# A two-block transformer kernel on one Trainium2 core: the second mixer's value products, all eight chunks of the first half of tokens ahead of the second half

## The chip, the core and the metric

The kernel runs as one program on one core of a Trainium2 chip. The core has engines that run side by side, each through its own list of instructions in order: TensorE (PE in the rows below; its loading of weights is PEld) multiplies matrices into PSUM, VectorE (DVE) and ScalarE (ACT) work elementwise, GpSimd (POOL) does a few small jobs, and SyncE (SP) issues the DMAs that bring weights from HBM to SBUF. Semaphores tie the lists together. The metric is device time of one execution in microseconds (us), the median of several; lower is better.

## The reference

The input is 256 tokens of width 1024. A first block (a recurrent mixer, a sparse attention and a gated embedding) is followed by two layers of the same form, `i` = 0 and 1:

```
mod = (silu(c) @ mod_w[i] + mod_b[i]) as six vectors of 1024
y   = mixer(x * (1 + mod[1]) + mod[0])            # i = 0: MLA, i = 1: MoBA
x   = layer_norm(ALPHA * x + mod[2] * y)
y   = conv_ffn(x * (1 + mod[4]) + mod[3])
x   = layer_norm(ALPHA * x + mod[5] * y)
```

The mixer of layer 1 (MoBA, with one block of 256 keys here) is causal attention with 8 heads of 128, with queries, keys and values from one 1024x3072 weight. What this document is about lies between the feed-forward part of layer 0 and the heads of layer 1: the layer norm between them, the values of the second mixer, and two of the modulation vectors, `mod[4]` and `mod[3]` of layer 1, which nobody needs before the layer norm behind the second mixer.

## The kernel before, in words

Every activation is kept as two parts, high and low, whose sum is the float32 value, and so is every weight. A weight chunk is 128 input channels by 1024 columns. Its DMA puts two chunks (1 MB) into one of six buffers `raw`. ACT makes the high part (`split`, L174), DVE the low part (L175), into one of four pairs of buffers `wh` and `wl`; with more than four chunks in a group, both parts of the others share a buffer `ws`, which is taken from the six of `raw`. A product of tokens by weight then costs three matmuls (`mm3t`, L213 to L215): high by high, high by low, and low by high, so L215 alone needs the low part of the activation.

**Halves.** Tokens go through a layer in two halves of 128, `tb` = 0 and 1. `tokens` calls `halves` once for each group of chunks; `halves` makes the splits of the whole group and then issues the matmuls, first all of the group for the first half, then for the second. The value products of the second mixer (`mobav`) had the groups [0, 1, 2, 3], [4, 5] and [6, 7]. Eight chunks, two halves, two column blocks of 512 and three terms make 96 matmuls.

**The layer norm in front.** When the feed-forward products of a half (`ps_fy`) are done, DVE adds the residual and takes the moments (L1084 to L1087), POOL makes the inverse deviation, DVE and ACT normalize half a row each (L1114, L1115). `feed` then turns the result into the mixer's input chunk by chunk: PE transposes (L367), ACT writes the high part `ln` (L372) and, for every second chunk, the scaled value (L376; DVE for the others, L374), DVE writes the low part (L377). `Norm.emit` says in which order: chunks 0 to 3 of the first half when that half is ready, and everything else after the second half is ready.

**Modulation units.** A modulation vector is four units of work, each with a DMA of 1 MB (`raw_mod`), and an end (`fin`: a sum with the bias in `modr`, two transposes `ps_modt`, a copy `mod`). A unit is done on PE (`mm`: eight matmuls of 32 rows by 256 columns, L983) or on DVE (`add`: four passes over 1024 columns, the first one of a vector on ACT, L996 and L998); if a vector had units on DVE, four more matmuls with `ones` bring their sum `modacc` into the same PSUM tile. `bg` takes the next unit from a queue. `fetch` and `units`, called by `halves` with `fill`, load some units early. Before, `fill` was 5 at the end of layer 0's feed-forward part: the last unit of `mod[4]` and all four of `mod[3]` of layer 1. The heads of the second mixer call `bg` once a step as long as `mod[3]` is missing.

The order of the instructions on each engine is set by a scheduler when the kernel is built; it keeps dependencies and the `issue_after` edges of the code, and otherwise moves work.

Of the kernel before, what the change touches and what calls it, by code (L numbers as in the profile page):

```python
# [21 lines left out]
KD = D // P  # L22
F = 2816
NF = F // P
# [23 lines left out]
class G:  # L48
# [7 lines left out]
    def __init__(self, ctx, tc, a):  # L56
        self.tc, self.nc, self.a = tc, tc.nc, a
        pool = lambda n, **kw: ctx.enter_context(tc.tile_pool(name=n, bufs=1, **kw))
        self.cp = pool("cp")
        self.sp = pool("stream")  # L60
        self.rp = pool("res")
        self.pp = pool("pp", space=PSUM)
        self.dp = pool("dp", space=DRAM)
        self.modrow = {}
        self.pending, self.marks, self.fed = None, [], {}
        self.queue, self.early, self.have = [], [], set()
# [960 lines left out]
def affine(g, name, gain, shift, scale, offset):  # L1027

    V = g.nc.vector
    s1, b1 = g.col(8, name + "s"), g.col(8, name + "b")  # L1030
    V.scalar_tensor_tensor(s1, scale, 1.0, gain, op0=ALU.add, op1=ALU.mult)
    if shift is None:
        V.tensor_copy(b1, offset)
    else:
        V.scalar_tensor_tensor(b1, scale, 1.0, shift, op0=ALU.add, op1=ALU.mult)
        V.tensor_tensor(b1, b1, offset, op=ALU.add)
    return s1, b1


class Norm:  # L1040


    def __init__(self, g, name, joint=False):
        self.g, self.name, self.joint = g, name, joint
        self.x = g.xs(name)
        self.r = [None, None]

    def emit(self, g, xh, tb, aff):
        self.r[tb] = xh
        lo, hi = list(range(4)), list(range(4, KD))  # L1050
        if self.joint:
            todo = [((0, 1), lo + hi)] if tb else []
        else:
            todo = [((1,), lo), ((0,), hi), ((1,), hi)] if tb else [((0,), lo)]
        for tbs, ks in todo:
            g.feed(self.r, tbs, ks, *aff, self.x, self.name)
# [18 lines left out]
def residual_moments(g, name, z, acc, cols, scale, after):  # L1075

    V = g.nc.vector
    st, mv = g.col(18, f"{name}st"), g.col(2, f"{name}mv")
    with ExitStack() as ctx:
        for ins in after:  # L1080
            ctx.enter_context(g.tc.issue_after(ins.ins))
        for n, c in enumerate(cols):
            t = g.b2(f"{name}t{n}")[:, 0:c.stop - c.start]
            V.tensor_tensor(t, acc(n), scale[:, c], op=ALU.mult)  # L1084
            V.scalar_tensor_tensor(z[:, c], z[:, c], ALPHA, t, op0=ALU.mult, op1=ALU.add)
            V.bn_stats(st[:, 6 * n:6 * n + 6], z[:, c])
        V.bn_aggr(mv, st[:, 0:6 * len(cols)])  # L1087
    return mv[:, 0:1], mv[:, 1:2]


def rstd(g, name, var):
    v = g.col(1, f"{name}v")
    g.nc.vector.tensor_scalar(v, var, LN_EPS, None, op0=ALU.add)
    return g.rsqrt(v, f"{name}r")


def resid_ln(g, i, j, prev, nxt, name):

    nc, a = g.nc, g.a
    V, A = nc.vector, nc.scalar  # L1100
    scale = g.row(g.modrow[i, (2, 5)[j]], name + "m")
    gain, shift = (g.row(a[n][i, j:j + 1, :], name + n) for n in ("ln_g_2", "ln_b_2"))
    out = Norm(g, name, j == 0)
    aff = affine(g, name + "a", g.ln_g[:, i, j, :], g.ln_b[:, i, j, :], *nxt)

    def done(tb, acc):
        z, h = prev[tb], f"{name}{tb}"
        cols = TAIL if tb and out.joint else N512
        after = g.marks if tb and not out.joint else ()
        mean, var = residual_moments(g, h, z, lambda n: acc(tb, n), cols, scale, after)  # L1110
        r = rstd(g, h, var)
        nr = g.col(1, f"{h}nr")
        iv = V.scalar_tensor_tensor(nr, mean, -1.0, r, op0=ALU.mult, op1=ALU.mult)
        V.tensor_scalar(z[:, 0:512], z[:, 0:512], mean, r, op0=ALU.subtract, op1=ALU.mult)  # L1114
        A.activation(z[:, 512:1024], z[:, 512:1024], AF.Identity, bias=nr, scale=r)  # L1115
        if out.joint == bool(tb):
            g.marks = [iv]
        out.emit(g, z, tb, aff)

    out.rows = gain, shift  # L1120
    return out, done
# [201 lines left out]
def moba(g, x, ln, early):  # L1323
    nc, a = g.nc, g.a
    A, T, V = nc.scalar, nc.tensor, nc.vector
    w = a["moba_w_in_2"][0]

    vacc = g.pair("mobav")
    vt = [g.b4(f"mobav{tb}") for tb in range(2)]

    def vdone(tb):
        for n, c in enumerate(N512):
            A.copy(vt[tb][:, c], vacc(tb, n))

    g.tokens(w, x, [[0, 1, 2, 3], [4, 5], [6, 7]], vacc, vdone, "mobav", c0=2048)
    g.flush()
    rest = early()
    q, k = [], []

    def units():  # L1340
        for hp in range(4):
            for m, ps in g.proj(w, 256 * hp, 2, x, f"mobaq{hp}", wide=True):
                q.append(g.t1(f"mobaq{2 * hp + m}"))
                g.added(ps, f"mobaq{2 * hp + m}", q[-1], 128.0 ** -0.5 * 2.0 ** (2 * hp + m + 1))
                yield
            for m, ps in g.proj(w, 1024 + 256 * hp, 2, x, f"mobak{hp}", wide=True):
                k.append(g.t1(f"mobak{2 * hp + m}"))
                g.added(ps, f"mobak{2 * hp + m}", k[-1])
                yield

    proj = units()
    for _ in range(5):
        next(proj)

    def fill(st):
        for _ in range(2):
            next(proj, None)
        if st >= 1 and rest:
            rest.pop(0)(g.smr)
        if (1, 3) not in g.have:  # L1360
            g.bg()

    def logits(h, out, tb):
        n = (tb + 1) * P
        T.matmul(out, q[h][:, tb * P:n], k[h][:, 0:n], start=True, stop=True)

    o = heads(g, "moba", logits, g.dist, lambda h: 2.0 ** -(h + 1), vt, "V", fill)
    n, done = ln()
    acc = g.pair("mobay")
    part = lambda tb, n: acc(tb, n, (N512, TAIL)[tb][n].stop - (N512, TAIL)[tb][n].start)  # L1370
    g.tokens(a["moba_w_o_2"][0], o, [[0, 1], [2, 3], [4, 5, 6, 7]], part, lambda tb: done(tb, part), "mobay", fill=4, by_column=True)
    return n


def ffn(g, i, x, ln, early):
    nc, a = g.nc, g.a
    V, A = nc.vector, nc.scalar
    w, wo = a["ffn_w_in_2"][i], a["ffn_w_out_2"][i]
    cw, cb = g.ffc[i], g.ffb[i]
    hid = [None] * NF  # L1380
# [39 lines left out]
    todo = [0, 2]  # L1420
    last = NF - (6, 8)[i]
    acc = g.pair(f"fy{i}", third="V")
    width = N512, TAIL if i else N512
    part = lambda tb, n: acc(tb, n, width[tb][n].stop - width[tb][n].start)
    load = g.loader(wo, 0, D, f"fo{i}_")
    ends = 0, NF - 1
    for c in range(4, NF, 2):
# [26 lines left out]
        if c == NF - 4:  # L1454
            n, done = ln()
        while todo[0] < min(c, last):
# [1 line left out]
            ks = [k for k in (m, m + 1) if k < last]  # L1458
            g.halves(load, ks, hid, part, width, f"fo{i}_", ends)
            todo = todo[1:]  # L1460
    g.halves(load, list(range(last, NF)), hid, part, width, f"fo{i}_", ends, lambda tb: done(tb, part), 0 if i else 5, i == 1)
    return n


# [55 lines left out]
```

## Time and profile before

| what | before |
|---|---|
| median of 3 runs | 877.28 us (877.24 to 877.99) |
| the profiled execution's own time | 879.18 us |
| its span, first to last instruction | 877.4 us |
| PE busy | 859.3 us, 98% |
| DVE busy | 673.2 us, 77% |
| ACT busy | 502.6 us, 57% |
| DMA read from HBM | 197.28 MB, 226 GB/s over the span |

The span is what the rows below measure in; 1.8 us of the execution's own time lie around it. Times in rows count from the span's start. Idle time of an engine stands in square brackets with what ended it. "PEclk" is the share of full speed that TensorE's clock was granted: 1.00 is 2.4 GHz, 0.50 is 1.2 GHz.

### The profile page before, as it was taken

The numbers are of one execution on the slowest core, as the hardware profiler recorded it, in microseconds if no ns is written. First come the engines' busy times: TensorE is split into PE (matmuls) and PEld (weight loads), VectorE is DVE, ScalarE is ACT, GpSimd is POOL, SyncE is SP. The second block draws the span as 40 slices with busy tenths as digits, with TensorE's granted clock in tenths as the row PEclk, the third lists the DMA queues.
The fourth block names the chain that finished last, engine by engine and source line by source line (L and its number), as shares of the span: only waits on it lengthen the run. The fifth ranks groups of instructions, "written<-read, shape, count | busy, mean of one in ns | idle before, by whom it ended". The sixth has DMA issues, their size and how long they took to land. (4 is left out here: it accounts for less than half of the span.)

```text
span 877.4 us, 14288 instructions
## 1 busy us (share of the span) xinstructions
PE 859.3 (98%) x5415; PEld 741.1 (84%) x5415; DVE 673.2 (77%) x1289; ACT 502.6 (57%) x925; POOL 52.6 (6%) x81
## 2 busy tenths in 40 slices
PE   9999999999999899999999999999999999999996
PEld 8998779999888688798888888678888988888885
DVE  5798787768767576679899998675866686777786
ACT  6555666445557555377556557276553775565660
POOL 2003111000000131000000000000000000000003
PEclk9999999999999999999999999999999999999999
DMA  8955796854447963498898985498453956566411
GB/s 269 357 197 175 279 345 202 285 211 151 144 150 258 305 250 117 132 377 286 305 331 296 336 290 190 162 345 296 161 176 104 377 178 203 181 220 204 143 49 48
DMA packets 112760, 199.27 MB, mean 227 GB/s; under 512 B 8388, under 2 KB 76468, under 8 KB 112692
## 3 DMA queue, kind: packets, MB, share of 16 engines
q1 hardware_dynamic: 111892, 196.25, 65.7%
q0 software_dynamic: 496, 1.59, 0.5%
q8 instruction: 42, 0.69, 0.3%
q10 hardware_dynamic: 304, 0.53, 0.2%
q14 instruction: 26, 0.21, 0.1%
HBM read 197.28 MB, written 1.08 MB: 226 GB/s over the span
## 5 line engine op out<-in xcount | busy, mean ns | idle before, releaser
L194 PE MATMUL ps_f<-ln,wh_f 128*128 128x512 f32 x576 | 203.8, 396 | 0.0
L195 PE MATMUL ps_f<-ln,wl_f 128*128 128x256 f32 x576 | 161.4, 280 | 0.0
L194 PEld LDWEIGHTS ps_f<-ln,wh_f 128*128 128x128 f32 x576 | 108.1, 188 | 26.5 <-issue 0.8
L195 PEld LDWEIGHTS ps_f<-ln,wl_f 128*128 128x128 f32 x576 | 108.7, 189 | 1.4 <-issue 0.4
L174 ACT CAST wh_fo<-raw_fo 128x1024 fp32r<-128x1024 f32 x38 | 39.9, 1050 | 39.3 <-PE ps_f L194 38.2
L174 ACT CAST wh_f<-raw_fa 128x1024 fp32r<-128x1024 f32 x36 | 37.7, 1051 | 40.8 <-PE ps_f L194 20.3
L175 DVE TENSOR_TENSOR wl_fo<-raw_fo,wh_fo 128x1024 fp32r<-128x1024 f32 x38 | 46.5, 1223 | 19.0 <-ACT wh_fo L174 18.9
L175 DVE TENSOR_TENSOR wl_f<-raw_fa,wh_f 128x1024 fp32r<-128x1024 f32 x36 | 43.9, 1222 | 15.3 <-ACT wh_f L174 15.3
L174 ACT CAST wh_f<-raw_fb 128x1024 fp32r<-128x1024 f32 x36 | 37.1, 1050 | 28.0 <-PE ps_fy L215 17.8
L998 DVE SCALAR_TENSOR_TENSOR modacc<-raw_mod,c,modacc 128x1024 f32<-128x1024 f32 x40 | 51.1, 1278 | 2.0 <-ACT modacc L996 2.0
L175 DVE TENSOR_TENSOR wl_f<-raw_fb,wh_f 128x1024 fp32r<-128x1024 f32 x36 | 43.4, 1221 | 9.2 <-ACT wh_f L174 8.9
L188 PE MATMUL ps_fi<-ln,wh_fi 128*128 128x256 f32 x128 | 35.6, 285 | 0.0
L215 PE MATMUL ps_fy<-wh_fo,fh 128*128 128x512 f32 (+1 forms) x99 | 35.2, 369 | 0.0
L214 PE MATMUL ps_fy<-wl_fo,fh 128*128 128x512 f32 (+1 forms) x99 | 35.1, 368 | 0.0
L189 PE MATMUL ps_fi<-ln,wl_fi 128*128 128x256 f32 x128 | 34.6, 283 | 0.0
L187 PE MATMUL ps_fi<-ln,wh_fi 128*128 128x256 f32 x128 | 34.0, 286 | 0.0
L213 PE MATMUL ps_fy<-wh_fo,fh 128*128 128x512 f32 (+1 forms) x99 | 33.3, 367 | 0.0
L204 DVE TENSOR_TENSOR adf<-ps_f,adf 128x256 f32<-128x256 f32 x72 | 30.0, 417 | 0.0
L983 PE MATMUL ps_mod<-raw_mod,c 128*32 128x256 f32 x400 | 26.9, 383 | 1.0 <-DVE mod L1013 1.0
L203 ACT COPY adf<-ps_f 128x256 f32<-128x256 f32 x72 | 26.1, 363 | 0.0
L174 ACT CAST wh_fi<-raw_fi 128x1024 fp32r<-128x1024 f32 x16 | 17.0, 1079 | 14.9 <-PE ps_mlay L215 8.3
L188 PEld LDWEIGHTS ps_fi<-ln,wh_fi 128*128 128x128 f32 x128 | 24.5, 192 | 0.4 <-DVE ln L377 0.4
(807 smaller groups left out, 2582.4 us busy)
## 6 DMA issues: line engine op xcount, KB each, us to landing
raw_mod<-in_mod_w_dram SPq DMA_DIRECT2D x48, 1024.0 KB
raw_fo<-in_ffn_w_out_dram SPq DMA_DIRECT2D x22, 1024.0 KB
raw_fa<-in_ffn_w_in_dram SPq DMA_DIRECT2D x18, 1024.0 KB
raw_fb<-in_ffn_w_in_dram SPq DMA_DIRECT2D x18, 1024.0 KB
raw_fi<-in_ffn_w_in_dram SPq DMA_DIRECT2D x16, 512.0 KB
raw_wo<-in_w_out_dram SPq DMA_DIRECT2D x6, 1024.0 KB
raw_aqk<-in_w_in_dram SPq DMA_DIRECT2D x4, 1024.0 KB
raw_mqk<-in_w_in_dram SPq DMA_DIRECT2D x4, 1024.0 KB
```

The lines of the kernel that those rows point to most:

```text
L174: self.nc.scalar.copy(hv, src)
L175: self.nc.vector.tensor_tensor(lv, src, hv.bitcast(F32), op=ALU.subtract)
L187: T.matmul(ps, wh, xh, start=start, stop=False, skip_group_check=chk)
L188: T.matmul(ps, wh, xl, start=False, stop=False, skip_group_check=chk)
L189: T.matmul(ps, wl, xh, start=False, stop=stop, skip_group_check=chk)
L194: T.matmul(ps, wh, x[2], start=start, stop=False, skip_group_check=True)
L195: T.matmul(ps[:, 0:S], wl, x[0], start=False, stop=stop, skip_group_check=True)
L204: V.tensor_tensor(t, ps[:, 0:S], t, op=ALU.add)
L213: T.matmul(ps, xh, wh, start=start, stop=False)
L214: T.matmul(ps, xh, wl, start=False, stop=False)
L215: return T.matmul(ps, xl, wh, start=False, stop=stop)
L998: nc.vector.scalar_tensor_tensor(st["acc"], rv[:, e], c, st["acc"], op0=ALU.mult, op1=ALU.add)
```

## The change

Three edits. The value products become one group of eight chunks, so all 48 matmuls of the first half stand ahead of those of the second, and chunks 4 to 7 of the weight are kept in `ws` buffers. The layer norm in front feeds each half whole, as soon as that half is ready. And of the five modulation units at the end of the feed-forward part one stays; the other four (`mod[3]`) go to the first four steps of the heads, by turns on DVE and on PE.

```diff
@@ class Norm
-    def __init__(self, g, name, joint=False):
-        self.g, self.name, self.joint = g, name, joint
+    def __init__(self, g, name, joint=False, whole=False):
+        self.g, self.name, self.joint, self.whole = g, name, joint, whole
...
         if self.joint:
             todo = [((0, 1), lo + hi)] if tb else []
+        elif self.whole:
+            todo = [((tb,), lo + hi)]
         else:
             todo = [((1,), lo), ((0,), hi), ((1,), hi)] if tb else [((0,), lo)]
@@ def resid_ln
-    out = Norm(g, name, j == 0)
+    out = Norm(g, name, j == 0, j == 1)
@@ def moba
-    g.tokens(w, x, [[0, 1, 2, 3], [4, 5], [6, 7]], vacc, vdone, "mobav", c0=2048)
+    g.tokens(w, x, [list(range(KD))], vacc, vdone, "mobav", c0=2048)
...
         if (1, 3) not in g.have:
-            g.bg()
+            g.bg(tensor=st % 2 == 1)
@@ def ffn
-    g.halves(..., lambda tb: done(tb, part), 0 if i else 5, i == 1)
+    g.halves(..., lambda tb: done(tb, part), 0 if i else 1, i == 1)
```

Two lines are added ahead of these places, so a line of the kernel before has a number two higher in the changed one from L1054 on.

How this moves instructions. On PE, right behind the last feed-forward product, before (`ps_mod` are modulation units, `ps_ln` the transposes of the feed, `x_72` and `x_73` the two halves):

```order
L215 MATMUL ps_fy_4894<-ws_fo_21_6224,fo_21l 128x512
L983 MATMUL ps_mod_6349<-raw_mod_6227,c 32x256 x6
L367 MATMUL ps_ln_6292<-ident,x_72 128x128 x4
L983 MATMUL ps_mod_6349<-raw_mod_6227,c 32x256 x2
L983 MATMUL ps_mod_6349<-modacc_5899,ones 32x256 x4
L1011 MATMUL ps_modt_6791<-ident,modr_6787 128x128 x2
L983 MATMUL ps_mod_6796<-raw_mod_6229,c 32x256 x8
L983 MATMUL ps_mod_6796<-raw_mod_6231,c 32x256 x8
L983 MATMUL ps_mod_6796<-raw_mod_6233,c 32x256 x8
L983 MATMUL ps_mod_6796<-raw_mod_6235,c 32x256 x3
L367 MATMUL ps_ln_6425<-ident,x_73 128x128 x4
```

and in the changed kernel, at the same place:

```order
L983 MATMUL ps_mod_6362<-modacc_5899,ones 32x256 x3
L213 MATMUL ps_mobav_6409<-wh_mobav_6375,ln_6066 128x512
L214 MATMUL ps_mobav_6409<-wl_mobav_6376,ln_6066 128x512
L213 MATMUL ps_mobav_6413<-wh_mobav_6375,ln_6066 128x512
L214 MATMUL ps_mobav_6413<-wl_mobav_6376,ln_6066 128x512
L1011 MATMUL ps_modt_6779<-ident,modr_6775 128x128 x2
L215 MATMUL ps_mobav_6409<-wh_mobav_6375,ln_6066 128x512
L215 MATMUL ps_mobav_6413<-wh_mobav_6375,ln_6066 128x512
L213 MATMUL ps_mobav_6409<-wh_mobav_6379,ln_6066 128x512
L214 MATMUL ps_mobav_6409<-wl_mobav_6380,ln_6066 128x512
L213 MATMUL ps_mobav_6413<-wh_mobav_6379,ln_6066 128x512
L214 MATMUL ps_mobav_6413<-wl_mobav_6380,ln_6066 128x512
```

Ahead of these rows stand one unit, one matmul with `ones` and eight transposes of the first half. Four units are gone, and the value products begin; the first low-part matmuls (L215) stand behind the two transposes of `modr`.

On DVE, behind the normalizing of the first half (`x_72`), before; `ln_6066` is the low part of chunk 0 and then of chunk 1:

```order
L1114 TENSOR_SCALAR x_72<-x_72,ln010mv,ln010ry 128x512
L1084 TENSOR_TENSOR ln011t_6408<-ps_fy_4887,row_ln01m 128x512
L1085 SCALAR_TENSOR_TENSOR x_73<-x_73,ln011t_6408 128x512
L1084 TENSOR_TENSOR ln011t_6412<-ps_fy_4894,row_ln01m 128x512
L1086 BN_STATS ln011st<-x_73 128x6
L1085 SCALAR_TENSOR_TENSOR x_73<-x_73,ln011t_6412 128x512
L1008 SCALAR_TENSOR_TENSOR modr_6787<-ps_mod_6349,modb_6788 128x256
L1086 BN_STATS ln011st<-x_73 128x6
L377 TENSOR_TENSOR ln_6066<-ln01f_6297,ln_6066 128x128
```

and in the changed kernel, from there to the low part of chunk 0:

```order
L1116 TENSOR_SCALAR x_72<-x_72,ln010mv,ln010ry 128x512
L175 TENSOR_TENSOR wl_mobav_6380<-raw_mobav_6373,wh_mobav_6379 128x1024
L175 TENSOR_TENSOR wl_mobav_6386<-raw_mobav_6383,wh_mobav_6385 128x1024
L175 TENSOR_TENSOR wl_mobav_6390<-raw_mobav_6383,wh_mobav_6389 128x1024
L1086 TENSOR_TENSOR ln011t_6461<-ps_fy_4887,row_ln01m 128x512
L1086 TENSOR_TENSOR ln011t_6465<-ps_fy_4894,row_ln01m 128x512
L175 TENSOR_TENSOR ws_mobav_6395<-raw_mobav_6393,ws_mobav_6395 128x1024
L175 TENSOR_TENSOR ws_mobav_6398<-raw_mobav_6393,ws_mobav_6398 128x1024
L1008 SCALAR_TENSOR_TENSOR modr_6775<-ps_mod_6362,modb_6776 128x256
L1087 SCALAR_TENSOR_TENSOR x_73<-x_73,ln011t_6461 128x512
L377 TENSOR_TENSOR ln_6066<-ln01f_6289,ln_6066 128x128
```

Five weight splits now stand between the normalizing and that low part. (One more stands ahead of the moments' `BN_AGGR` of the first half.) The rows that follow in the changed kernel, to the low part of chunk 1:

```order
L1087 SCALAR_TENSOR_TENSOR x_73<-x_73,ln011t_6465 128x512
L374 TENSOR_SCALAR ln01f_6293<-ps_ln_6284,ln01as,ln01ab 128x128
L175 TENSOR_TENSOR ws_mobav_6403<-raw_mobav_6401,ws_mobav_6403 128x1024
L175 TENSOR_TENSOR ws_mobav_6406<-raw_mobav_6401,ws_mobav_6406 128x1024
L1013 COPY mod_6782<-ps_modt_6779 128x2x4
L1088 BN_STATS ln011st<-x_73 128x6 x2
L377 TENSOR_TENSOR ln_6066<-ln01f_6293,ln_6066 128x128
```

The last two splits and the moments of the second half stand ahead of it; before, four short rows lie between those two low parts.

## Rows read from the trace of the kernel before

**Rows 1.** The page's first part: busy time, share of the span, instructions.

```profile
PE 859.3 (98%) x5415; PEld 741.1 (84%) x5415; DVE 673.2 (77%) x1289; ACT 502.6 (57%) x925; POOL 52.6 (6%) x81
```

**Rows 2.** Stretches: length, busy time (instructions) by engine, PEclk, DMA share, GB/s.

```profile
562.85:572.88 10.03, 8.76 (x108) 4.77 (x107) 7.12 (x21) 5.63 (x11) 0.55 (x1) 1.00 0.95 340
572.88:594.99 22.11, 22.11 (x98) 18.05 (x98) 15.16 (x28) 16.26 (x29) 0.00 (x0) 1.00 1.04 345
609.00:650.20 41.20, 41.20 (x252) 36.75 (x251) 32.44 (x84) 25.49 (x57) 0.00 (x0) 1.00 0.53 180
650.20:682.40 32.20, 31.41 (x216) 24.98 (x214) 19.62 (x48) 11.93 (x25) 1.21 (x2) 1.00 0.39 132
```

**Rows 3.** Timeline of PE: start, length, instruction, count, idle before.

```profile
562.62 0.40 PE L215 MATMUL ps_fy<-ws_fo,fo_21l 128*128 128x512 f32 x1
...
567.29 3.22 PE L983 MATMUL ps_mod<-raw_mod,c 128*32 128x256 f32 x54 [0.74 <-DVE mod L1013]
570.44 1.53 PE L367 MATMUL ps_ln<-ident,x 128*128 128x128 f32 x12
571.90 1.05 PE L983 MATMUL ps_mod<-raw_mod,c 128*32 128x256 f32 x10
...
594.99 0.62 PE L194 MATMUL ps_mobaq<-ln,wh_mobaq 128*128 128x512 f32 x2
```

**Rows 4.** SP's issues and ACT around the first value weights, same columns.

```profile
550.39 0.37 SPq L159 DMA_DIRECT2D raw_mod<-in_mod_w_dram  x1
...
563.04 0.37 SPq L159 DMA_DIRECT2D raw_mobav<-in_moba_w_in_dram  x1
...
564.63 0.46 ACT L372 ACTIVATE ln<-ps_ln,ln01ab,ln01as 128x128 fp32r<-128x128 f32 x1 [4.39 <-PE ps_ln L367]
...
570.38 1.99 ACT L174 CAST wh_mobav<-raw_mobav 128x1024 fp32r<-128x1024 f32 x2 [0.98 <-DMA raw_mobav<-in_moba_w_in_dram]
```

**Rows 5.** The DMA engines from 556.5 to 562.3, columns of rows 2.

```profile
556.50:562.30 5.80, 5.80 (x27) 4.71 (x26) 3.27 (x8) 0.81 (x1) 0.55 (x1) 1.00 0.00 0
```

**Rows 6.** Groups by line, 562.8 to 595: count, busy, mean ns, idle before.

```profile
L175 DVE TENSOR_TENSOR wl_mobav<-raw_mobav,wh_mobav 128x1024 fp32r<-128x1024 f32 x8 | 9.6, 1220 | 1.8 <-ACT wh_mobav L174 1.8
...
L983 PE MATMUL ps_mod<-raw_mod,c 128*32 128x256 f32 x80 | 6.0, 383 | 0.7 <-DVE mod L1013 0.7
...
L1333 ACT COPY mobav<-ps_mobav 128x512 f32<-128x512 f32 x3 | 1.7, 590 | 1.7 <-PE ps_mobav L215 1.7
```

**Rows 7.** Timeline of DVE over the same place, columns of rows 3.

```profile
554.45 1.29 DVE L1084 TENSOR_TENSOR ln010t<-ps_fy,row_ln01m 128x512 f32<-128x512 f32 x2 [2.07 <-PE ps_fy L215]
555.66 1.28 DVE L1085 SCALAR_TENSOR_TENSOR x<-x,ln010t 128x512 f32<-128x512 f32 x2
556.86 1.28 DVE L1086 BATCH_NORM_STATS2 ln010st<-x 128x6 f32<-128x512 f32 x2
...
559.31 0.54 DVE L1114 TENSOR_SCALAR x<-x,ln010mv,ln010ry 128x512 f32<-128x512 f32 x1
...
565.62 0.42 DVE L1008 SCALAR_TENSOR_TENSOR modr<-ps_mod,modb 128x256 f32<-128x256 f32 x1 [0.69 <-PE ps_mod L983]
...
566.57 0.27 DVE L377 TENSOR_TENSOR ln<-ln01f,ln 128x128 fp32r<-128x128 f32 x1
566.76 0.40 DVE L374 TENSOR_SCALAR ln01f<-ps_ln,ln01as,ln01ab 128x128 f32<-128x128 f32 x1
...
571.46 2.36 DVE L175 TENSOR_TENSOR wl_mobav<-raw_mobav,wh_mobav 128x1024 fp32r<-128x1024 f32 x2 [1.82 <-ACT wh_mobav L174]
```

**Rows 8.** PE in the first mixer, after its longest wait: timeline, then one stretch.

```profile
299.30 0.50 PE L213 MATMUL ps_mlv<-wh_ukv,ckh 128*128 128x512 f32 x1 [2.63 <-ACT krx L1221]
...
302.33 0.63 PE L215 MATMUL ps_mlv<-wh_ukv,ckl 128*128 128x512 f32 x1
302.76 0.63 PE L213 MATMUL ps_mlv<-wh_ukv,ckh 128*128 128x512 f32 x1
...
300.33:303.75 3.42, 3.42 (x9) 2.64 (x9) 2.96 (x6) 0.80 (x2) 2.51 (x4) 0.50 1.11 328
```

**Rows 9.** The page's costliest groups: a modulation pass on DVE.

```profile
L998 DVE SCALAR_TENSOR_TENSOR modacc<-raw_mod,c,modacc 128x1024 f32<-128x1024 f32 x40 | 51.1, 1278 | 2.0 <-ACT modacc L996 2.0
```

More of the change, by code (lines that the diff above doesn't have):

```diff
@@ L1460, in ffn @@
             todo = todo[1:]
-    g.halves(load, list(range(last, NF)), hid, part, width, f"fo{i}_", ends, lambda tb: done(tb, part), 0 if i else 5, i == 1)
+    g.halves(load, list(range(last, NF)), hid, part, width, f"fo{i}_", ends, lambda tb: done(tb, part), 0 if i else 1, i == 1)
     return n
```

## The prediction

> **What bounds the kernel now.** I read the busy shares first: PE is busy 859.3 us, 98% of the span, DVE 77%, ACT 57% [rows 1]. So work taken off PE is worth its full length and work put on it costs its full length, except in the few places where PE stands still. The question is where this change finds idle time of PE, and where it makes some. The table of stretches, second, splits the neighbourhood of the change [rows 2]. From the last feed-forward product to the first value product (562.85 to 572.88) PE is busy 8.76 of 10.03 us. The value products behind it are busy 22.11 of 22.11. In the heads (609.0 to 650.2) PE is busy 41.20 of 41.20 while DVE is at 32.44 and ACT at 25.49. Only behind them, to 682.4, is there slack again: 32.20 less 31.41 is 0.79. The timelines of PE, then SP and ACT, say why PE doesn't start the value products earlier: its ten microseconds are filled with modulation units [rows 3], whose loads held the raw buffers. The first value load is issued at 563.04, as a buffer comes free, and its first cast at 570.38 waited for that DMA [rows 4]. From 556.5 to 562.3 the DMA engines moved nothing [rows 5].
>
> **What the change removes.** Five units are 80 records of PE [rows 6], 40 matmuls, since each shows twice. The 54 records from 567.29 take until the transposes at 570.44, 3.15 us [rows 3]; 16 records, one unit, are 0.93. Four units less are 3.7 us off these ten, and three `ones` matmuls go with them or change place. The value load of six chunks can be issued where the units' loads were (one is at 550.39 [rows 4]), so it no longer binds. The fourth MB still waits for a buffer that the last feed-forward product frees, so it is issued near 563.0. By the rate of 345 GB/s of the value stretch [rows 2] it needs 3.0 us; the first value load of before took 7.3 with others behind it [rows 4]. I take 568 to 569, between the two.
>
> **What is late next.** The order shows that all eight splits of the weight (L175) now stand on DVE ahead of the second low part of the feed (L377). A split's mean is 1.220 us [rows 6]; two in a row last 2.36 [rows 7], so each further one costs 1.14. Before, normalizing ends at 559.31 + 0.54 = 559.85 [rows 7]. Now one split stands ahead of it: 561.0. Three more splits, 3.42: 564.4. Two L1084, at 1.29 a pair some 1.2 in a queue: 565.6. Two splits, 2.28: 567.9. The sum with the bias (L1008, 0.3 to 0.42): 568.2. One L1085, 0.6, and L377, 0.2: the low part of chunk 0 is there at 569.0, where before it took no split at all (566.57 + 0.27 [rows 7]). Behind it come L1085 0.6, L374 0.4, two splits 2.28, L1013 0.1 and two L1086 1.2: the low part of chunk 1 is there at 573.7. A landing of the last MB at 566 leaves this as it is; one at 570.4 adds two casts of 1.0 [rows 4] and a split and makes it 575.1.
>
> **PE against that.** It begins at 562.9. One unit 0.93, one `ones` matmul 0.12, eight transposes at 0.12 (12 take 570.44 to 571.90 [rows 3]) 0.98, the copy of the first `ln` by ACT 0.4: 565.3. Four products without a low part, at 22.11 / 96 = 0.230 each [rows 2], 0.92: 566.2. The transposes of `modr` wait for L1008, until 568.2: 2.0 idle. They take 0.2, and then L215 waits until 569.0: 0.5 idle. Six products of chunk 0 and the beginning of chunk 1, 1.4: 570.4. L215 of chunk 1 waits until 573.7: 3.3 idle. The 38 products that are left of the first half, 8.75: 582.5. At the seam stand eight transposes, 0.98, and a wait for ACT, which copies an accumulator (0.59 [rows 6]) and then `ln` (0.46 [rows 4]): some 0.3. Then 48 products, 11.05: 594.8. Before, the last one ended at 594.99 [rows 3]. So the stage gains 0.2 at full clock: 3.7 of units and 1.3 of idle time and what is saved of `ones`, and it waits 5.8 + 0.3. Its bounds: +1.4 later by the late landing, and 6.0 earlier if DVE held up nothing.
>
> **The clock.** Before, the two idle pieces in this stretch (0.74 is the longer [rows 3]) left the granted clock at 1.00 [rows 2]. After PE's longest wait in the first mixer, 2.63 us, the clock was 0.50 from 300.33 to 303.75, 3.42 us, and products stood 0.43 apart (302.33 to 302.76) instead of 0.23 [rows 8]. That costs half of the stretch, 1.7. Waits of 2.0, 0.5 and 3.3 within eight microseconds are more idle than that one wait, so I take one such stretch, +1.7; the bounds are 0 and two of them, 3.4. The first burst at half clock would be hidden, as PE waits for DVE behind it anyhow.
>
> The Trainium skill, "TensorE: Matmul & The Clock Gate", section "HAM oscillation — how this bites in real kernels", describes a kernel whose waits throttle the engine again between bursts, so that every burst starts cold. By that rule the seam's wait or the wait before would bring a second stretch. Rows 8 show one stretch behind one long wait and no second; this second is among the rivals.
>
> **The units that move.** Two run on PE in the heads, 2 x 0.93 = 1.86, and each of the four `ones` matmuls that bring DVE's sum into PSUM costs 0.12, as a transposition does, 0.47 together. PE has no idle time there [rows 2]: +2.35, bounds 1.9 (if the `ones` only replace those of the removed group) and 3.0. Two run on DVE and ACT: three passes at 1.278 [rows 9], 3.8, and one on ACT of about that length, beside 8.8 us that DVE and 15.7 that ACT have free [rows 2]; I cost them at nothing. If a pass stands ahead of a split or a softmax step for which PE waits, up to 1.3 each come back. Their four MB come in during a stretch that moves 180 GB/s where 345 were reached [rows 2]: 3.0 us a MB, 12 of 41, hidden unless a buffer comes free late. Behind the heads to 682.4 the end of the scheduler's order changes with the buffers; there is 0.79 to gain or, as nothing in the trace shows otherwise, as much to lose. I take 0. The normalizing feed of the first half, whole now, has PE's transposes in the same number: 0.
>
> **Sum.** -0.2 + 1.7 + 2.35 + 0 = +3.85. The profiled execution, 877.4 of span and 1.8 around, becomes 883.0; it is 1.9 above the median of the runs shown, so the median goes from 877.28 to 881.1.
>
> **Rivals.**
> Clock holds: PE's waits come as above, but in pieces that leave the clock at 1.00, as in rows 2. 881.1 - 1.7 = 879.4. For it speak the two short pieces of before; against it rows 8.
> Clock falls twice: the 3.3 us wait and the seam each bring a stretch. 882.9. Against it, the seam's wait is short.
> Loads late in the heads: the units' four MB take buffers from the query and key weights, and a PE that has no idle time now waits for one of them, 1.5 to 2.5: 883. For it: six buffers, four of which the value products keep to their end. Against it: 180 of 345 GB/s.
> Half the stalls: the splits run earlier than in my chain, in DVE's free time of 556.5 to 562.3 (3.27 busy of 5.80 [rows 5]); the stalls with their clock cost are 3.7 us instead of 7.5 and the change comes out even, near 877.3.
> Faster: DVE holds PE up nowhere, since seven splits are done before the first half is normalized. The value products run from 565.3 without a wait, 22.1 and the seam's 1.3 behind it: 588.9, 6.0 early, less 2.35 in the heads: 873.6. It decides from the point where stalls and clock together stay under 3.7. For it: the DMA engines and ACT (0.81 of 5.80) are free in that stretch [rows 5]. Against it: by the order four splits stand behind the normalizing and four only behind the residual of the second half, which cannot begin before the products end at 563.
>
> **How the numbers follow.** My chain with one stretch at half clock 0.47 (881.1; its own range 880.0 to 882.2); clock holds 0.18; clock twice 0.08; loads late 0.08; half the stalls 0.10; faster 0.09. Within 0.2% (1.75 us, 875.5 to 879.0, about what a measurement of this kernel tells from no change) lie half the stalls and a sixth of the clock-holds case: 0.13. Slower are the others, 0.78; faster 0.09. The range from 877.6 to 884.0 leaves out the faster case and most of the even one.
>
> **What would show it.** In the changed profile PE begins the value products near 565.3, not 572.9, and behind that shows waits of about 2.0, 0.5 and 3.3, put down to DVE (`modr`, `ln` L377). The first half's products end near 584 with the clock's loss, the second's near 596.5. A stretch of some 3.4 us has PEclk 0.50. The value stage up to the first query product ends 1.5 later than 594.99, and the heads are 2.35 longer, with PE still full. If PE's idle time between 563 and 584 is under 3, the chain on DVE is wrong; if it is as said but no record shows half clock, the clock's term is; if the heads grow by 4 or more, the hidden units or loads are.

## The result and the profile after

The changed kernel takes 883.71 us (median of 4 runs, 881.98 to 885.31) where the kernel before takes 877.59: a ratio of 1.0067, 95% interval 1.0055 to 1.0079. The forecast was slower, by 3.85 us to 881.1; it is slower by 6.1.

The profiled execution of the changed kernel took 883.82 us, with a span of 882.0. That is 4.64 above the profiled execution of before, and not 6.1, because that one had a half-clock stretch in the first mixer behind a wait of 2.63 us [rows 8]; the one of after waits 1.25 us there, keeps full clock, and comes to the end of layer 0's feed-forward part 1.7 us earlier. To keep this apart, the two traces are compared from an event that both have: the last feed-forward product of layer 0. It starts at 562.62 before [rows 3] and at 560.92 after.

First the busy times (share of the span, instructions), the lines that answer to [rows 1]:

```profile
PE 861.0 (98%) x5391; PEld 740.0 (84%) x5391; DVE 676.3 (77%) x1292; ACT 504.1 (57%) x926; POOL 52.7 (6%) x81
```

PE is busy 1.7 us longer [rows 1], with 24 instructions less. Next the stretches: length, then busy time (instructions) of PE, PEld, DVE, ACT and POOL, granted clock, DMA share, GB/s. The first reaches from the last feed-forward product to the first value product of the second half, the second from there to the last modulation matmul in front of the next layer norm, the third lies inside the first.

```profile
561.15:583.47 22.32, 17.81 (x92) 12.69 (x91) 14.02 (x32) 10.30 (x21) 0.55 (x1) 0.92 0.52 172
583.47:684.92 101.45, 100.86 (x619) 82.88 (x620) 68.04 (x155) 51.51 (x105) 1.06 (x2) 1.00 0.65 222
573.37:576.77 3.40, 3.40 (x9) 2.62 (x8) 1.82 (x6) 1.86 (x4) 0.30 (x1) 0.50 0.66 230
```

PE stands still for 4.51 of the first 22.32 us, where before it was busy from the first value product on [rows 2], and then works 3.40 us at half clock. Behind that there is next to no idle time, but the stretch is long: 101.45 us where the kernel before needs 96.4 to the same modulation matmul, at 680.33. (The kernel before mixes the two halves; its stretch is counted back from the first query product at 594.99 by 48 products of 0.23 us, to 583.94 [rows 2, 3].) PE's timeline shows the waits (start, length, instruction, count, idle time before it and what ended it):

```profile
560.92 0.40 PE L215 MATMUL ps_fy<-ws_fo,fo_21l 128*128 128x512 f32 x1
...
564.25 0.50 PE L213 MATMUL ps_mobav<-wh_mobav,ln 128*128 128x512 f32 x1
...
566.42 0.44 PE L1011 MATMUL ps_modt<-ident,modr 128*128 128x128 f32 x2 [0.98 <-DVE modr L1008]
567.22 0.74 PE L215 MATMUL ps_mobav<-wh_mobav,ln 128*128 128x512 f32 x2 [0.36 <-DVE ln L377]
...
571.88 0.73 PE L215 MATMUL ps_mobav<-wh_mobav,ln 128*128 128x512 f32 x2 [3.00 <-DVE ln L377]
...
574.21 0.63 PE L213 MATMUL ps_mobav<-wh_mobav,ln 128*128 128x512 f32 x1
574.64 0.63 PE L214 MATMUL ps_mobav<-wl_mobav,ln 128*128 128x512 f32 x1
...
583.47 0.50 PE L213 MATMUL ps_mobav<-wh_mobav,ln 128*128 128x512 f32 x1 [0.16 <-ACT ln L372]
```

The waits stand where the prediction put them, and the first three are put down to DVE: `modr`, the low part of chunk 0, the low part of chunk 1. At 574.21 the products stand 0.43 apart instead of 0.23. DVE's own timeline, same columns, says why; it answers to [rows 7], where no split stood between the normalizing and the first low parts:

```profile
558.62 0.54 DVE L1116 TENSOR_SCALAR x<-x,ln010mv,ln010ry 128x512 f32<-128x512 f32 x1
559.08 3.49 DVE L175 TENSOR_TENSOR wl_mobav<-raw_mobav,wh_mobav 128x1024 fp32r<-128x1024 f32 x3
562.48 1.28 DVE L1086 TENSOR_TENSOR ln011t<-ps_fy,row_ln01m 128x512 f32<-128x512 f32 x2
563.68 2.35 DVE L175 TENSOR_TENSOR ws_mobav<-raw_mobav,ws_mobav 128x1024 fp32r<-128x1024 f32 x2
565.95 0.42 DVE L1008 SCALAR_TENSOR_TENSOR modr<-ps_mod,modb 128x256 f32<-128x256 f32 x1
566.28 0.68 DVE L1087 SCALAR_TENSOR_TENSOR x<-x,ln011t 128x512 f32<-128x512 f32 x1
566.88 0.29 DVE L377 TENSOR_TENSOR ln<-ln01f,ln 128x128 fp32r<-128x128 f32 x1
567.08 0.69 DVE L1087 SCALAR_TENSOR_TENSOR x<-x,ln011t 128x512 f32<-128x512 f32 x1
567.68 0.41 DVE L374 TENSOR_SCALAR ln01f<-ps_ln,ln01as,ln01ab 128x128 f32<-128x128 f32 x1
568.01 2.35 DVE L175 TENSOR_TENSOR ws_mobav<-raw_mobav,ws_mobav 128x1024 fp32r<-128x1024 f32 x2
570.27 0.16 DVE L1013 COPY mod<-ps_modt 128x8 f32<-128x8 f32 x1
570.35 1.28 DVE L1088 BATCH_NORM_STATS2 ln011st<-x 128x6 f32<-128x512 f32 x2
571.54 0.48 DVE L377 TENSOR_TENSOR ln<-ln01f,ln 128x128 fp32r<-128x128 f32 x2
```

No row has idle time before it: from 558.6 to 572 DVE works without a pause, and 8.2 of these 13.4 us are splits.

### The profile page after: what moved, and what is told of

Same layout as the page of the kernel before. It is cut to its first block, busy times and chain, and to the rows that moved or that the text cites. A ratio compares the mean times of both kernels' runs of the same rounds, so it can differ in the third digit from the quotient of the medians.

```text
span 882.0 us, 14238 instructions
## 1 busy us (share of the span) xinstructions
PE 861.0 (98%) x5391; PEld 740.0 (84%) x5391; DVE 676.3 (77%) x1292; ACT 504.1 (57%) x926; POOL 52.7 (6%) x81
## 5 line engine op out<-in xcount | busy, mean ns | idle before, releaser
L998 DVE SCALAR_TENSOR_TENSOR modacc<-raw_mod,c,modacc 128x1024 f32<-128x1024 f32 x43 | 54.9, 1278 | 2.9 <-ACT modacc L996 2.7
L215 PE MATMUL ps_fy<-wh_fo,fh 128*128 128x512 f32 (+1 forms) x99 | 35.2, 369 | 0.0
```

The lines of the kernel that those rows point to most:

```text
L215: return T.matmul(ps, xl, wh, start=False, stop=stop)
L998: nc.vector.scalar_tensor_tensor(st["acc"], rv[:, e], c, st["acc"], op0=ALU.mult, op1=ALU.add)
```

## The experiments

Each kernel was timed against the kernel before in runs on the same chip. "Offset" is the time from the last feed-forward product of layer 0 to the last modulation transposes before the next layer norm, read from the profile: 120.36 us before (562.62 to 682.98), 126.65 after (560.92 to 687.57). It leaves out what the clock did in the first mixer. Its ends, before and after:

```profile
682.98 0.38 PE L1011 MATMUL ps_modt<-ident,modr 128*128 128x128 f32 x2
```

```profile
687.57 0.38 PE L1011 MATMUL ps_modt<-ident,modr 128*128 128x128 f32 x2
```

| kernel | us, median (before beside it) | ratio, 95% interval | offset |
|---|---|---|---|
| changed kernel | 883.71 (877.59) | 1.0067 (1.0055 to 1.0079) | 126.65 |
| units edit alone | 878.39 (877.54) | 1.0013 (1.0004 to 1.0022) | 121.22 |
| group and feed alone | 882.89 (877.54) | 1.0063 (1.0050 to 1.0076) | 125.80 |
| changed, late splits | 879.25 (877.54) | 1.0025 (1.0015 to 1.0034) | 122.05 |
| changed, units on DVE | 879.16 (877.54) | 1.0022 (1.0012 to 1.0031) | 121.88 |
| before, units on DVE | 873.85 (877.78) | 0.9959 (0.9947 to 0.9972) | 116.58 |
| changed, both steps | 875.77 (877.78) | 0.9975 (0.9964 to 0.9986) | 118.11 |
| changed, 22 matmuls in the wait | 884.89 (877.78) | 1.0077 (1.0065 to 1.0089) | 126.66 |
| before, units on PE in the heads | 879.66 (877.78) | 1.0025 (1.0016 to 1.0035) | 122.59 |
| changed, 12 matmuls in the wait | 882.13 (877.33) | 1.0059 (1.0046 to 1.0071) | 125.15 |
| before, no unit in front | 874.27 (877.33) | 0.9966 (0.9954 to 0.9978) | 117.12 |
| whole feed alone | 878.47 (877.33) | 1.0009 (1.0000 to 1.0019) | 120.15 |

**The units edit alone.**

```diff
-    ... lambda tb: done(tb, part), 0 if i else 5, i == 1)
+    ... lambda tb: done(tb, part), 0 if i else 1, i == 1)
-            g.bg()
+            g.bg(tensor=st % 2 == 1)
```

> The third edit alone: one modulation unit in front of the value products, the other four by turns on DVE and PE in the heads; the groups [0..3], [4, 5], [6, 7] and the feed stay as in the kernel before. Theory A (the loss of the changed kernel in its value stage is DVE's: four more weight splits ahead of the low parts): without those splits PE waits under 1.5 us between the last feed-forward product and the value products, no stretch at half clock falls there, and the value products end some 5 us earlier than before; the heads and what follows cost 4 to 5 us as in the changed kernel: 876 to 877.5 us. Theory B (what the heads and the tail cost beyond the 2.35 forecast comes from buffers that the eight-chunk group holds): the stage wins the same and the rest costs only 2.35: 874 to 875.

Measured 878.39, above both. Its PE timeline has one wait in the value stage, and the first query product comes early:

```profile
560.93 0.40 PE L215 MATMUL ps_fy<-ws_fo,fo_21l 128*128 128x512 f32 x1
...
567.61 0.73 PE L215 MATMUL ps_mobav<-wh_mobav,ln 128*128 128x512 f32 x2 [0.73 <-DVE ln L377]
...
588.60 0.61 PE L194 MATMUL ps_mobaq<-ln,wh_mobaq 128*128 128x512 f32 x2
...
682.15 0.38 PE L1011 MATMUL ps_modt<-ident,modr 128*128 128x128 f32 x2
```

So the stage from the last feed-forward product to the first query product takes 27.67 us instead of 32.37, 4.7 less: early weights without the eight-chunk group's splits do pay. What follows takes 93.55 instead of 87.99, 5.56 more. The same loss stands behind the value stage in the changed kernel (101.45 - 96.4 = 5.05), so held buffers of the eight-chunk group (theory B) are not its cause.

**The group and the feed alone.**

```diff
-    out = Norm(g, name, j == 0)
+    out = Norm(g, name, j == 0, j == 1)
-    g.tokens(w, x, [[0, 1, 2, 3], [4, 5], [6, 7]], vacc, vdone, "mobav", c0=2048)
+    g.tokens(w, x, [list(range(KD))], vacc, vdone, "mobav", c0=2048)
```

> The first two edits alone: one group of eight chunks, each half fed whole, and all five modulation units in front of the value products as before. Theory A (the first two edits hurt only because the weights then come early and their splits stand ahead of the low parts): the weights come late as before, DVE's low parts come ahead of all splits, no wait over 1 us: 876.5 to 878.5 us. Theory B (the order of the products by itself costs the time, by the wait at the seam between the halves or by splits that come too late for eight chunks in a row): 879.5 us or more, with PE waits inside the first half's products.

Theory A fell and theory B holds: 882.89. Three pieces of its timeline: PE's waits, one of ACT's casts of the weights, and SP's issue of the last load:

```profile
576.40 0.73 PE L213 MATMUL ps_mobav<-wh_mobav,ln 128*128 128x512 f32 x2 [1.30 <-ACT wh_mobav L174]
578.18 0.51 PE L214 MATMUL ps_mobav<-wl_mobav,ln 128*128 128x512 f32 x1 [1.04 <-DVE wl_mobav L175]
581.89 0.50 PE L214 MATMUL ps_mobav<-ws_mobav,ln 128*128 128x512 f32 x1 [0.69 <-DVE ws_mobav L175]
585.28 0.73 PE L213 MATMUL ps_mobav<-ws_mobav,ln 128*128 128x512 f32 x2 [0.83 <-ACT ws_mobav L174]
586.54 0.50 PE L214 MATMUL ps_mobav<-ws_mobav,ln 128*128 128x512 f32 x1 [0.52 <-DVE ws_mobav L175]
```

```profile
584.18 2.00 ACT L174 CAST ws_mobav<-raw_mobav 128x1024 fp32r<-128x1024 f32 x2 [2.19 <-DMA raw_mobav<-in_moba_w_in_dram]
```

```profile
577.47 0.42 SPq L159 DMA_DIRECT2D raw_mobav<-in_moba_w_in_dram  x1
```

Eight chunks for one half are eaten at 6 x 0.23 = 1.4 us each; with both halves in turn a chunk lasted twice as long. The weights, behind five units' loads, come slower than that: the last is issued only at 577.47, as a buffer comes free. The waits add up to 4.4 us, of the 5.4 by which the offset grows; the other 1.0 was not traced. The group needs early weights, and early weights with the group's splits block DVE.

**The changed kernel with its last splits held back.**

```diff
             with ExitStack() as ctx:
                 if k != ends[0]:
                     self.after_marks(ctx)
+                if name == "mobav" and k >= 4:
+                    ctx.enter_context(self.tc.issue_after(self.fed[3][1].ins))
```

> The changed kernel, with the splits of chunks 4 to 7 held back behind the low part of chunk 3 of the first half. Theory A (PE waits for DVE, on which the splits of chunks 4 to 7 stand ahead of the low parts, and the half clock follows from that wait): the idle 4.5 us of PE between 563 and 583 falls to about 1.3, no half clock follows in most runs: 3.2 + 1.7 less, 878 to 879.5 us. Theory B (something else holds PE, such as ACT or the landing of the last weights): the wait moves to chunk 4 and the time stays at 883 to 884.

Theory A holds: 879.25, 4.5 less than the changed kernel. The waits left, of PE:

```profile
567.83 0.73 PE L215 MATMUL ps_mobav<-wh_mobav,ln 128*128 128x512 f32 x2 [0.73 <-DVE ln L379]
568.80 0.51 PE L213 MATMUL ps_mobav<-wh_mobav,ln 128*128 128x512 f32 x1 [0.24 <-ACT ln L374]
575.54 1.09 PE L369 MATMUL ps_ln<-ident,x 128*128 128x128 f32 x8 [1.14 <-DVE x L1118]
```

They are 2.1 us, not the 1.3 expected: one of 1.14 came to the second half's transposes. Its profile has no half clock there.

**The changed kernel with all units on DVE.**

```diff
-            g.bg(tensor=st % 2 == 1)
+            g.bg(tensor=False)
```

> The changed kernel, with all four moved units on DVE and ACT in the heads, none on PE. Theory A (PE's cost of two units in the heads is their 16 matmuls and about 0.3 us at each change between the small modulation matmuls and the large ones): 2.5 to 3.5 us less, 880 to 881 us. Theory B (DVE, with eight more passes of 1.28 us, becomes late for the weight splits and the softmax of the heads): PE waits in the heads, and the time stays at 883 or rises.

Theory A's direction, more than its size: 879.16, 4.55 less for two units. Its waits in the value stage are those of the changed kernel (3.01 before chunk 1, and half clock behind it), and its offset is 4.8 shorter, 4.5 of it behind the first product of the second half: nearly all of the gain lies in the heads and behind them. No wait of PE for DVE came with the eight more passes.

**The kernel before with one unit in front and the rest on DVE.** Groups and feed as before.

```diff
-    ... lambda tb: done(tb, part), 0 if i else 5, i == 1)
+    ... lambda tb: done(tb, part), 0 if i else 1, i == 1)
-            g.bg()
+            g.bg(tensor=False)
```

> The kernel before, with one modulation unit in front of the value products and all four others on DVE and ACT in the heads; old groups, old feed. Theory A (two independent terms: early weights shorten the value stage by 4.5 us as in the run with the units edit alone, and what was lost behind it, 5.4 us, came mostly from the two units on PE): 878.4 less the 4.5 us that the changed kernel won by the same step: 873.5 to 875 us, faster than the kernel before by about 0.4%. Theory B (the gain of that step in the changed kernel came out of PE's waits there, which this kernel doesn't have): 877 us or more.

Theory A holds: 873.85, the fastest kernel of this study, 0.41% faster than the kernel before. (Its profiled run took 876.58: it has two half-clock stretches, at 181 and 301 us, both ahead of what is compared here.) The stretch from the first query product to the last modulation matmul, in the kernel before, with the units by turns, and with the units on DVE (three kernels, columns as above):

```profile
594.99:680.33 85.34, 84.94 (x532) 72.69 (x531) 58.87 (x137) 43.27 (x90) 1.05 (x2) 1.00 0.54 179
```

```profile
588.60:679.50 90.90, 90.31 (x572) 73.75 (x571) 62.28 (x141) 44.12 (x91) 1.06 (x2) 1.00 0.57 199
```

```profile
591.10:677.38 86.28, 85.98 (x540) 72.87 (x539) 65.88 (x145) 43.91 (x91) 1.04 (x2) 1.00 0.61 209
```

Length and PE's busy time go together in all three: PE is full. In the third, DVE carries 7.0 us more than before, and the stretch is 0.94 longer, 0.6 of it `ones` matmuls that the kernel before does not need there. Two units on PE make 90.90 - 86.28 = 4.6 us, 2.3 each, where a unit in a row takes 0.93.

**Both steps on the changed kernel.** The splits of chunks 4 to 7 held back as above, and

```diff
-            g.bg(tensor=st % 2 == 1)
+            g.bg(tensor=False)
```

> The changed kernel with both steps: the splits of chunks 4 to 7 behind the low part of chunk 3, and all four units on DVE in the heads. Theory A (the two terms are independent): 879.25 - 4.5 = 874.7, 874 to 875.5 us. Theory B (the two share a cause, DVE's queue): 877 us or more. Against the run with the old groups it tells whether eight chunks in a row are worth anything once nothing waits: by A they are worth 0 or less.

875.77, a little above theory A's range and below B: of the 4.5 and 4.55 that the two steps gain alone, 7.9 are gained together, so the two terms are nearly independent. Eight chunks in a row with the whole feed and the late splits are 1.9 us slower than the old groups (873.85). Something still waits there: PE's waits are 0.71 before chunk 1 and 1.14 for the second half's normalizing, where the kernel with the old groups has 0.73 alone. What eight chunks in a row are worth without any wait stays open.

**Small matmuls in the long wait, 22 and then 12.**

```diff
+ # mobav, first half, chunk 1: L213 and L214 for both columns, then
+ with self.tc.issue_after(ins.ins):
+     for e in range(22):
+         ins = T.matmul(acc(1, 0)[:, 0:P], self.ident, self.ident, start=True, stop=True)
+ # then, issued after these, L215 for both columns
```

> The changed kernel with 22 small matmuls on PE (identity by identity, into an accumulator that is not in use yet), placed between the four products of chunk 1 that have no low part and the two that wait for it: PE then works, for nothing, through most of the 3.0 us for which it waits for DVE. Theory A (the wait makes the clock fall, and that costs 1.7 us): no stretch at half clock behind 571, 881.5 to 882.3 us median. Theory B (the clock falls for another reason, or DVE's lateness costs the same again later): a stretch of 3.4 us at half clock stays, 883.4 us or more.

> The changed kernel with 12 small matmuls on PE in its longest wait, where the run with 22 had too many: those took 0.22 us each, 4.8 in all, and ran 1.7 us past the end of the wait, while the clock stayed at 1.00. Twelve take 2.6 of the 3.0 us. Theory A (the wait makes the clock fall, and that costs 1.7 us): no half clock behind 571, and 881.7 to 882.4 us median. Theory B (the clock is not what costs the time): 883.4 us or more, as the changed kernel.

The first one missed its aim: 884.89. Each of the 22 took 0.22 us, two records of 0.11, where I had reckoned with a transpose's 0.12. They ended 1.7 us past the wait, as much as the clock gave back: the offset is that of the changed kernel. With 12 the median is 882.13, 1.6 under the changed kernel, and the offset 1.5 under it. The kernels before in the two sets of runs differ by 0.26, and the two intervals overlap, so the medians alone would not decide it. The profile has no half clock there:

```profile
568.72 2.84 PE L284 MATMUL ps_mobav<-ident 128*128 128x128 f32 x24
571.89 0.73 PE L287 MATMUL ps_mobav<-wh_mobav,ln 128*128 128x512 f32 x2 [0.34 <-DVE ln L390]
572.46 0.40 PE L213 MATMUL ps_mobav<-wh_mobav,ln 128*128 128x512 f32 x1
572.70 0.39 PE L214 MATMUL ps_mobav<-wl_mobav,ln 128*128 128x512 f32 x1
```

The low part still comes at the same moment (571.89), the idle piece in front of it is 0.34, and the products behind stand 0.23 apart. So what the stage gains is the clock's, 1.5 by the offset and 1.7 by the length of the stretch. The runs of the changed kernel agree: mean granted clocks of 0.998, 0.995, 0.995 and 0.993 go with spans of 880.2, 881.8, 882.0 and 883.5 us, and the one at 0.998 took 881.98, where four of the five runs with 12 matmuls lie (881.89 to 882.31). One of these four kept its clock with the wait as it is, so a single profile could be the same chance; all runs together make that unlikely. With the wait of 3.0 us unfilled (the changed kernel, and the one with all units on DVE) 13 of 14 runs have mean clocks of 0.993 to 0.996; with 22 or 12 matmuls in it six of ten have 0.997 or 0.998.

**The kernel before with one unit in front and the rest on PE.** The heads keep `g.bg()`.

```diff
-    ... lambda tb: done(tb, part), 0 if i else 5, i == 1)
+    ... lambda tb: done(tb, part), 0 if i else 1, i == 1)
```

> The kernel before with one modulation unit in front of the value products and all four others on PE in the heads (no pass on DVE, so no matmuls with ones). Theory A (each unit on PE in the heads costs its 16 records at 1.36 us and about 0.7 us in the products next to it, the ones-matmuls 0.93 in all): against the run with the units by turns on DVE and PE (878.4), two units more and the ones less: 880.5 to 882 us. Theory B (what costs is DVE's part: its passes and the ones): under 878.4.

879.66, between the two. It is slower than with the units by turns, so DVE's part is not the cost; but two more units on PE cost 1.3 net of the `ones` matmuls, not the 2.1 to 3.6 expected. A unit's price on PE in the heads is not one number: 2.3 for the first two, about 0.9 to 1.1 for the next two, with the `ones` put back at 0.47 or 0.93. The trace says why. Add up PE's time record by record, from each start to the next start, behind the first query product. The units' own records take 2.72 more with two units on PE than with none (1.36 a unit) and 4.10 more here, for the 52 of the 64 records that stand there (1.26 a unit). The products of the heads and of the output around them take 1.5 more with two units and 1.1 more here. That second part does not grow with the number of units.

**No unit in front.** Against the fastest kernel:

```diff
-    ... lambda tb: done(tb, part), 0 if i else 1, i == 1)
+    ... lambda tb: done(tb, part), 0, i == 1)
```

> The faster kernel of the last call (old groups, units on DVE), with the last modulation unit in front of the value products gone as well: all five on DVE and ACT in the heads. Theory A (PE's work in front of the value products counts in full): one unit, 0.93 to 1.0 us, less, its sum's wait gone too, some 0.5 us for another four matmuls with ones saved or added: 872.3 to 873.3 us. Theory B (PE then waits for the low part of chunk 0 instead, which DVE has at about the same moment as now): 873.5 to 874.2, the same as with the unit.

874.27, at the upper end of theory B: the unit in front costs nothing, since PE then waits instead:

```profile
561.94 0.50 PE L213 MATMUL ps_mobav<-wh_mobav,ln 128*128 128x512 f32 x1 [0.55 <-ACT ln L372]
...
563.65 0.73 PE L215 MATMUL ps_mobav<-wh_mobav,ln 128*128 128x512 f32 x2 [0.52 <-DVE ln L377]
```

**The whole feed alone.**

```diff
-    out = Norm(g, name, j == 0)
+    out = Norm(g, name, j == 0, j == 1)
```

> The second edit alone: each half is fed whole as soon as it is ready, old groups, five units in front as before. Theory A (the feed's order is no term of its own as long as the units stand there): within 1 us of the kernel before, 877 to 878.5 us. Theory B (the first half's eight chunks on DVE and ACT make the second half's late): 879 us or more.

878.47, within theory A's range, with an interval that touches no change, and an offset 0.2 below the one before: the feed's order is no term of this result.

## Why the prediction was right, and where its size was off

**The number.** 883.71 lies in the stated range (877.6 to 884.0), by 0.3 us, and above the 880.0 to 882.2 that the prediction gave its own chain. The rivals near it are loads late in the heads (883) and a second half-clock stretch (882.9), and the profile shows neither. That the range still held is luck; the direction and the mechanism in the value stage are not, as the next parts show.

**DVE's chain: right.** From the start of the last feed-forward product the prediction has `modr` 5.6, the low part of chunk 0 6.4 and that of chunk 1 11.1 us later. Measured: 5.45 (566.37 - 560.92), 6.25 (567.17) and some 10.9. The late-splits kernel shows that the order is the cause: with the splits of four chunks held back, the wait of 3.00 falls to 0.73.

**PE's waits: right place, smaller.** 0.98, 0.36, 3.00 and 0.16 instead of 2.0, 0.5, 3.3 and 0.3. The first is smaller because PE began the products 3.3 us after the last feed-forward product and not 2.7: the `ones` matmuls stand in front of them, four and not one. This changed no end, since DVE sets the moment at which the products go on. The list with which the prediction explains its gain of 0.2 (3.7 of units, 1.3 of idle time and the `ones` against 6.1 of waits) adds up to a loss of some 0.6; its chain of times gives the gain, and the chain is what the trace bears out.

**The clock: right.** 3.40 us at 0.50, once, 1.7 us, as taken from [rows 8]; in the profiled run no second stretch followed, so the rival with two falls away. The Trainium skill ("TensorE: Matmul & The Clock Gate", section "HAM oscillation — how this bites in real kernels") has a kernel that is throttled again after each of its long waits. This trace agrees for the one long wait, of 3.00 us. What did not hold is the step that the prediction made from there to short waits: those of 0.98, 0.36 and 0.16 left the clock at full speed. In one of the four runs (881.98) the mean clock of 0.998 leaves no room for a stretch at half clock.

**The value stage** as a whole: to the first product of the second half 22.55 us (560.92 to 583.47) against 21.32 before (562.62 to 583.94), +1.23 where -0.2 + 1.7 = 1.5 were forecast. The weights landed early enough: the first cast of chunk 4 ended its wait for the DMA at 566.40.

**The units in the heads: the step that was mis-sized.** The prediction put 2.35 us on "the units that move", bounds 1.9 and 3.0, and nothing on what lies behind the heads, where it allowed 0.8 either way. Measured is 5.05 (101.45 - 96.4). Taking the two units off PE gives 4.55 back in the changed kernel, and 4.54 in the kernel with old groups (878.39 - 873.85); what then remains over the kernel before is 0.94 (680.03 - 591.10 = 88.93 against 87.99), of which the `ones` take 0.57. So the missing 2.7 come with the two units on PE, though not as a wait: PE's idle time in the stretch is 0.59. The prediction's sign for this case, heads that grow by 4 or more, blamed the hidden units or the loads. Both are cleared: with all four units on DVE only 0.6 to 0.9 of the growth is left, and PE waits for no DMA there.

One part can be read in the timeline. The units' price of 0.93 came from a row of 54 records without a break [rows 3]; in the heads the scheduler cuts units into short bursts between larger products:

```profile
618.06 0.28 PE L195 MATMUL ps_mobak<-ln,wl_mobak 128*128 128x256 f32 x1
618.27 1.05 PE L983 MATMUL ps_mod<-raw_mod,c 128*32 128x256 f32 x10
619.26 0.50 PE L194 MATMUL ps_mobaq<-ln,wh_mobaq 128*128 128x512 f32 x1
...
622.06 0.28 PE L195 MATMUL ps_mobaq<-ln,wl_mobaq 128*128 128x256 f32 x1
622.27 0.63 PE L983 MATMUL ps_mod<-raw_mod,c 128*32 128x256 f32 x6
622.83 0.55 PE L1177 MATMUL ps_mobapt<-ident,mobapr 128*128 128x128 f32 x3
...
633.16 0.28 PE L195 MATMUL ps_mobak<-ln,wl_mobak 128*128 128x256 f32 x1
633.37 0.62 PE L983 MATMUL ps_mod<-raw_mod,c 128*32 128x256 f32 x2
633.92 0.50 PE L194 MATMUL ps_mobaq<-ln,wh_mobaq 128*128 128x512 f32 x1
```

A product of the first form takes 0.11, so the ten records hold PE from 618.17 to 619.26, 1.09 us, where ten in a row take 0.58; six hold it 0.66 instead of 0.35, and two 0.65 instead of 0.12. The fourth burst, the last 14 records with the eight of the `ones`, holds it from 636.84 to 638.37, 1.53 instead of 1.28. The four bursts so cost 1.6 more than the same records in a row. The rest stands in products that are the same in both kernels. Added up record by record, from each start to the next, they take 1.5 us more in the changed kernel than with all units on DVE: 0.56 in the output products (`ps_mobay`), 0.54 in the queries and keys, 0.42 in the other products of the heads. (0.4 of this is the product right ahead of each burst, which the 1.6 holds too.) Which step makes these products take longer is open; no single wait carries it.

**The faster rival** failed where the prediction said it would: splits stand behind the normalizing, and DVE is full. They are seven there, as in the prediction's own chain, and not the four that the rival's text counts. But one half of its idea is true: with the old groups the early weights shorten the stage by 4.7 us, and with the units on DVE that is kept, 873.85. The rival "loads late in the heads" is out: PE has no wait there for a DMA. Half the stalls is out too: 4.5 us idle plus 1.7 are nearer to the chain's 7.5 than to 3.7.

**Sum.** +1.23 in the stage and +5.06 behind it are +6.29 between the two profiles' common events; less the 1.7 that the profile of before lost in the first mixer this is the 4.6 between their spans. That profile (879.18) lies 1.6 above the median of before, and the profile of after 0.1 above its own, so the medians differ by 6.1.

## What to carry to other kernels

A weight that is loaded earlier brings its split earlier too: look at what then stands behind it on the elementwise engine, before counting the gain of the load. What small matmuls cost depends on where they stand: on an engine that is full, ten of these records took 1.09 us in a burst between large products and 0.58 in an unbroken row, and the products around them took longer too. So time such a move with the rest of the kernel around it. Work that an engine with free time can do (here eight passes on DVE at 77% busy) was cheaper there, at several times the length: eight passes of 1.28 us in place of two units that cost PE 4.5.

## What the hardware showed that was not expected

One wait of 3.00 us of PE was followed by 3.40 us at half clock; 2.84 us of matmuls of no use in that wait, with 0.34 left idle, kept the clock at full speed in the profiled run and won some 1.6 us. In the first mixer PE waits for ACT at the same place in every kernel, for a time that differs from profile to profile: waits of 2.63 (before), 2.11 (before, units on DVE) and 1.85 us (group and feed alone) were followed by 3.4 us at half clock, waits of 1.06 to 1.36 us in the ten other profiles by none.

Such a stretch can also come without a wait. In two profiles (before with units on DVE, and the whole feed alone) the clock falls to half for some 3.4 us between 181.5 and 185.0 (0.51 and 0.52 over that stretch) with no idle time of PE in front, behind two bursts of small matmuls of 4 rows; the kernel before has the same bursts and 1.00 there.

A matmul of 128x128 in float32 with the identity took 0.22 to 0.24 us, two records, where a transpose of the same size in the same stage takes 0.12.
